# Attention's reciprocal sums: broadcast through memory instead of by matmul with the unit matrix

## The chip, the cores and the metric
The kernel runs on one core of one Trainium2 chip. The metric is the device time of one execution in microseconds, the median of several runs. PE is the matmul engine, DVE the vector engine, ACT the scalar engine, POOL the GpSimd engine, and SP the engine whose queue issues all transfers of this kernel.

## The reference, cut to what matters
One inference step of a hybrid diffusion backbone with two layers: first latent attention beside a convolution branch, then a bidirectional state space mixer. There are 256 context tokens and 1024 latent tokens; everything is fp32. The change concerns the attention of the first layer, 8 heads of width 64. Context queries see the 256 context keys, latent queries see 1536 (512 cached and 1024 own):

```python
s = (einsum('bqhd,bkhd->bhqk', qn, k_nope) + einsum('bqhr,bkr->bhqk', qr, k_rope)) * ATTN_SCALE
p = softmax(s, axis=-1)
attn = einsum('bhqk,bkhd->bqhd', p, v)
mix = concatenate([attn, cv], axis=-1) * silu(gate)
```

The softmax is computed as exp(s - max); the product with v is taken of the exponentials, and the result is multiplied by the reciprocal of each query's sum and by the gate.

## The kernel before
Attention works on head pairs p (4 of them) and query blocks b of 256 tokens (5; b = 0 is the context). A pair and a block make a group, 20 in all; a group has four units (j, qi): head j of the pair, 128 queries qi. All matmuls of scores are three fp32r products (lines 119 to 121, called from a helper), which stand for one product of full precision.

For each unit, u_scores makes the scores with the queries on partitions (one to three tiles of up to 512 keys), takes row maxima on DVE (line 617), the exponentials on ACT with their row sums (line 626), and the reciprocal of the sum, ri, one number for each partition (lines 630, 631, 633). One unit later, u_trans transposes the exponentials on PE (line 646), 128 keys at a time, and copies them out of PSUM (lines 650 and 652). u_values runs for a group after the first unit of the next group has been transposed: it multiplies with v (line 666), with the values' features on partitions and the queries along the row. There the reciprocals are needed along the row, the same on 64 partitions. Before the change PE makes this turn: for each of the four units the column ri, repeated 64 times, is the stationary operand, and the unit matrix is the moving one (line 661). The result goes to the second half of the PSUM tile of the group, po. Then DVE makes t2 = gate x reciprocals (line 671) and om = values x t2 (line 672), and om is stored (line 673). There is one po tile at a time.

Other work runs in this stretch. When the last unit of a pair is through its scores, prep_pair makes the next pair's keys and queries: it loads kh and kl (lines 570, 571) and query weights, and POOL makes the low part ql of the queries (line 588). A convolution branch, conv_norm, is fed in step by step and uses POOL for products and sums of up to 128x1024. The gate tile sg of a group is loaded ahead (line 705; two buffers, freed by t2). After attention the output projection follows on PE, in PSUM tiles that attention frees.

The order of the instructions on each engine isn't that of the text: the compiler's planner lays it out with a simulated timeline (schedule_with_timeline_sim=True in kernel()), and each engine, and SP's queue, then runs its list in order. An instruction that waits holds up those behind it on the same engine.

Of the kernel before, what the change touches and what calls it, by code (L numbers as in the profile page):

```python
# [10 lines left out]
F32 = mybir.dt.float32  # L11
# [39 lines left out]
def body(nc, tc, d, dbg=None, stop=None):  # L51
    es = ExitStack()
    with es:
        _body(nc, tc, d, es, dbg or {}, stop)


def _body(nc, tc, d, es, dbg, stop):
    V, S, G, PE = nc.vector, nc.scalar, nc.gpsimd, nc.tensor
    dma = nc.sync.dma_start

    def pool(name, bufs=1, space=None, side=None, stack=es):
        kw = {}
        if space is not None:
            kw["space"] = space
        if side is not None:
            kw["side"] = side
        if space is None:
            kw["reuse_waits"] = "tile"
        return stack.enter_context(tc.tile_pool(name=name, bufs=bufs, **kw))
# [5 lines left out]
    sm = pool("sm", bufs=3, side="left")  # L75
# [9 lines left out]
    dp = pool("dp", space=DRAM)  # L85

    def psum(tag="x"):
        tag = tag if tag in ptags else "sd"
        p, n = ptags[tag]
        return p.tile([128, 512], F32, name="ps" + tag, tag=tag, bufs=n)  # L90
# [5 lines left out]
    ident = cp.tile([128, 128], F32, name="ident")  # L96
# [21 lines left out]
    def mm3(ps, lh, ll, rh, rl, start, stop_):  # L118
        PE.matmul(ps, lh, rh, start=start, stop=False)  # L119
        PE.matmul(ps, lh, rl, start=False, stop=False)  # L120
        PE.matmul(ps, ll, rh, start=False, stop=stop_)  # L121
# [378 lines left out]
    ap_ = pool("attn", bufs=2, side="right", stack=esB)  # L500
# [92 lines left out]
    for p in range(4):  # L593
        for b in range(5):
            for j in range(2):
                for qi in range(2):
                    units.append((p, b, j, qi))

    def u_scores(u, kq):
        p, b, j, qi = u  # L600
        ks, qs = kq
        tok = (0 if b == 0 else 256 + 256 * (b - 1)) + 128 * qi
        ci = 0 if tok < 256 else (1 if tok < 768 else 2)
        o = tok - CHUNKS[ci][0]
        segs = [0] if b == 0 else [1, 2, 3]
        qh, ql = qs[(j, ci)]
        mx = sm.tile([128, 4], F32, name="mx", tag="mx", bufs=6)
        sums = sm.tile([128, 4], F32, name="sums", tag="sums", bufs=6)
        nk = sum(KSEG[si][1] for si in segs)
        prob = ap_.tile([128, 1536], F32, name="prob", tag="prob")  # L610
        pss = []
        for x, si in enumerate(segs):
            n = KSEG[si][1]
            kh, kl = ks[(j, si)]
            ps = psum("s")
            mm3(ps[:, :n], qh[:, o:o + 128], ql[:, o:o + 128], kh[:, :n], kl[:, :n], True, True)
            V.tensor_reduce(mx[:, x:x + 1], ps[:, :n], axis=AX.X, op=ALU.max, negate=len(segs) == 1)  # L617
            pss.append((ps, n))
        if len(segs) > 1:
            nm = sm.tile([128, 1], F32, name="nm", tag="nm", bufs=6)  # L620
            V.tensor_reduce(nm, mx[:, :len(segs)], axis=AX.X, op=ALU.max, negate=True)  # L621
        else:
            nm = mx[:, 0:1]
        c = 0
        for x, (ps, n) in enumerate(pss):
            S.activation(prob[:, c:c + n], ps[:, :n], AF.Exp, bias=nm, accum_out=sums[:, x:x + 1])  # L626
            c += n
        ri = sm.tile([128, 1], F32, name="ri", tag="ri", bufs=8)
        if len(segs) > 1:
            V.tensor_reduce(ri, sums[:, :len(segs)], axis=AX.X, op=ALU.add)  # L630
            V.reciprocal(ri, ri)
        else:
            V.reciprocal(ri, sums[:, 0:1])
        return prob, ri, nk

    def u_trans(u, st, pts):
        p, b, j, qi = u
        prob, ri, nk = st
        for g in range(0, nk // 128, 4):
            n4 = min(4, nk // 128 - g)  # L640
            if qi == 0:
                pts[(j, g)] = ap_.tile([128, 4, 256], F32, name="ptile", tag="pt", bufs=7)
            dst = pts[(j, g)]
            ps = psum("pt")
            for x in range(n4):
                PE.transpose(ps[:, x * 128:(x + 1) * 128], prob[:, (g + x) * 128:(g + x + 1) * 128], ident)  # L646
            o = dst[:, :n4, qi * 128:qi * 128 + 128]
            p3 = ps[:, :n4 * 128].rearrange("p (k q) -> p k q", q=128)
            if g == 4:
                V.tensor_copy(o, p3)  # L650
            else:
                S.copy(o, p3)  # L652
        pts[("r", j, qi)] = ri

    def u_values(p, b, pts):
        q0 = 0 if b == 0 else 256 + 256 * (b - 1)
        kts = list(range(2)) if b == 0 else list(range(2, 14))
        po = psum("po")
        for qi in range(2):
            for j in range(2):  # L660
                PE.matmul(po[64 * j:64 * j + 64, 256 + 128 * qi:384 + 128 * qi],
                          pts[("r", j, qi)].to_broadcast([128, 64]), ident, start=True, stop=True)
        for x, kt in enumerate(kts):
            for j in range(2):
                h = 2 * p + j
                PE.matmul(po[64 * j:64 * j + 64, 0:256], vt[:, kt, 64 * h:64 * h + 64],  # L666
                          pts[(j, 4 * (x // 4))][:, x % 4, :], start=x == 0, stop=x == len(kts) - 1)
        t2 = ap_.tile([128, 256], F32, name="t2", tag="t2")
        sg = sgs.pop((p, b))
        om = ap_.tile([128, 256], F32, name="om", tag="om")  # L670
        V.tensor_mul(t2, sg, po[:, 256:512])
        V.tensor_mul(om, po[:, 0:256], t2)
        dma(mixd[p, :, q0:q0 + 256], om)

# [25 lines left out]
    for i in range(len(units) + 2):  # L700
        if i < len(units):
            u = units[i]
            if i % 4 == 0:
                sgs[u[:2]] = ap_.tile([128, 256], F32, name="sg", tag="sg")
                dma(sgs[u[:2]], sgd[u[0], :, 256 * u[1]:256 * u[1] + 256])
            state[u] = u_scores(u, kqs[u[0]])
            if i % 20 == 19 and u[0] < 3:
                kqs[u[0] + 1] = prep_pair(u[0] + 1)
        if 0 < i <= len(units):
            v = units[i - 1]  # L710
            pts = done.setdefault((v[0], v[1]), {})
            u_trans(v, state.pop(v), pts)
            if v[2] == 1 and v[3] == 1:
                late_v.append(v)
        if i % 4 == 1 and late_v:
            v = late_v.pop(0)
            u_values(v[0], v[1], done.pop((v[0], v[1])))
        if ci < len(cn) and i % 20 in (1, 3, 5, 7, 9, 11, 13):
            next(cn[ci])
            ci += 1  # L720
        if i == 68:
            esE.close()
            esA.close()
            wps[0] = pool("wpB", bufs=2, side="left")
            hls.append(pool("hlB0", bufs=16, side="left", stack=esH))
            load_mix(0, KORD[:4])
            wao.extend(split_w(d["wao"][m], 8, 128) for m in range(2))
# [161 lines left out]
    def dtile(name, dt=F32, tag=None):  # L889
        return dq.tile([128, HT], dt, name=name, tag=tag or name)  # L890
# [40 lines left out]
    p = dtile("p")  # L931
# [43 lines left out]
    for half in range(2):  # L975
        hs = slice(half * 64, half * 64 + 64)
        for c0 in range(0, 5):
            c = half * 5 + c0
# [561 lines left out]
```

## Time and profile before

| | |
|---|---|
| median of 3 runs | 2057.92 us (2056.36 to 2061.26) |
| the profiled execution | 2060.95 us |
| its span, first to last instruction | 2059.1 us |
| PE busy, share of the span | 1993.4 us, 97% |
| DVE, ACT, POOL busy | 69%, 43%, 28% |
| mean granted clock of PE | 0.988 |
| attention, from the first scores to the last om | 381 to 797 us |

The profiled execution is one run; its time is the span and a little around it. Busy time of PE is the union of matmuls that overlap each other in the pipeline, so the times of single matmuls add up to more than the stretch that they take. The chain of waits goes back from the last instruction and puts each moment down to the one piece of work that everything then hung on.

### The profile page before, as it was taken

The numbers are of one execution on the slowest core, as the hardware profiler recorded it, in microseconds if no ns is written. First come the engines' busy times: TensorE is split into PE (matmuls) and PEld (weight loads), VectorE is DVE, ScalarE is ACT, GpSimd is POOL, SyncE is SP. The second block draws the span as 40 slices with busy tenths as digits, with TensorE's granted clock in tenths as the row PEclk, the third lists the DMA queues.
The fourth block names the chain that finished last, engine by engine and source line by source line (L and its number), as shares of the span: only waits on it lengthen the run. The fifth ranks groups of instructions, "written<-read, shape, count | busy, mean of one in ns | idle before, by whom it ended". The sixth has DMA issues, their size and how long they took to land.

```text
span 2059.1 us, 32474 instructions
## 1 busy us (share of the span) xinstructions
PE 1993.4 (97%) x11830; PEld 1626.0 (79%) x11830; DVE 1415.9 (69%) x2257; ACT 882.3 (43%) x1683; POOL 578.7 (28%) x487
## 2 busy tenths in 40 slices
PE   6999999999999999989999999999999999799997
PEld 3787888777777777868888888888888888589997
DVE  5798798556666673275757876876778587784744
ACT  5411321666566673244544343443334244333531
POOL 1211122212222311563123333333433243342001
PEclk8999999999999999999999999999999999999998
DMA  8434213311122224331566768765866678755442
GB/s 315 181 118 150 54 70 108 115 57 42 57 60 60 77 82 164 140 114 52 142 217 205 229 203 237 208 191 173 244 204 194 179 235 252 220 182 185 145 157 72
DMA packets 273341, 313.57 MB, mean 152 GB/s; under 512 B 21184, under 2 KB 221920, under 8 KB 273184
## 3 DMA queue, kind: packets, MB, share of 16 engines
q1 hardware_dynamic: 273184, 311.51, 48.0%
q8 instruction: 94, 1.54, 0.3%
q14 instruction: 63, 0.52, 0.1%
HBM read 223.38 MB, written 88.05 MB: 151 GB/s over the span
## 4 chain that ended last, share of the span: by engine, by line
PE 90%; DVE 3%; DMA 2%; ACT 1%; issue 1%; SPq 1%; POOL 0%; DVEq 0%; ACTq 0%; POOLq 0%
PE psmm L119 18%; PE psmm L120 18%; PE psmm L121 18%; PE pspo L666 5%; PE pspt L646 4%; PE pssd L1078 3%; PE pss L119 3%; PE pssd L1159 3%; PE pss L121 3%; PE pss L120 3%; PE pssd L1164 2%; PE pssd L1136 2%; PE pssd L1139 2%; PE psx L229 1%; PE pstm L1036 1%
## 5 line engine op out<-in xcount | busy, mean ns | idle before, releaser
L119 PE MATMUL psmm<-hl,wh 128*128 128x512 f32 (+1 forms) x1152 | 428.1, 372 | 4.7 <-ACT wh L114 3.5
L121 PE MATMUL psmm<-hl,wl 128*128 128x512 f32 (+1 forms) x1152 | 423.5, 368 | 4.3 <-POOL wl L115 4.3
L120 PE MATMUL psmm<-hl,wh 128*128 128x512 f32 (+1 forms) x1152 | 423.3, 367 | 0.0
L115 POOL TENSOR_TENSOR wl<-ws,wh 128x1024 fp32r<-128x1024 f32 x89 | 223.6, 2514 | 516.7 <-ACT wh L114 424.5
L119 PEld LDWEIGHTS psmm<-hl,wh 128*128 128x128 f32 x1152 | 219.1, 190 | 37.6 <-ACT wh L114 4.5
L121 PEld LDWEIGHTS psmm<-hl,wl 128*128 128x128 f32 x1152 | 218.8, 190 | 36.9 <-POOL wl L115 6.2
L120 PEld LDWEIGHTS psmm<-hl,wh 128*128 128x128 f32 x1152 | 218.8, 190 | 29.6 <-issue 0.7
L383 DVE SCALAR_TENSOR_TENSOR cacc<-cvin,acw,cacc 128x1295 f32<-128x1295 f32 x120 | 206.9, 1740 | 4.6 <-ACT cacc L378 3.1
L114 ACT CAST wh<-ws 128x1024 fp32r<-128x1024 f32 x109 | 113.6, 1043 | 199.6 <-PE psmm L120 140.3
L848 DVE SCALAR_TENSOR_TENSOR cy<-raw,prm,cy 128x1282 f32<-128x1282 f32 x96 | 157.2, 1637 | 24.6 <-ACT cy L845 17.0
L120 PE MATMUL psmm<-hlo,wh 128*128 128x512 f32 (+3 forms) x480 | 172.1, 359 | 0.0
L119 PE MATMUL psmm<-hh,wh 128*128 128x512 f32 (+3 forms) x480 | 167.8, 360 | 2.5 <-ACT hh L259 2.0
L121 PE MATMUL psmm<-hh,wl 128*128 128x512 f32 (+3 forms) x480 | 170.1, 357 | 0.0
L617 DVE TENSOR_REDUCE mx<-pss 128x1 f32<-128x512 f32 (+1 forms) x208 | 137.3, 668 | 35.2 <-PE pss L121 34.2
L1083 POOL TENSOR_TENSOR st<-st,dec_bc 128x256 f32<-128x256 f32 x104 | 84.3, 815 | 245.2 <-DVE st L1085 165.9
L119 PE MATMUL psmm<-yh,wh 128*128 128x256 f32 (+1 forms) x476 | 147.8, 314 | 5.2 <-ACT yh L1203 3.1
L120 PE MATMUL psmm<-yl,wh 128*128 128x256 f32 (+1 forms) x476 | 148.0, 312 | 0.4 <-DVE yl L1204 0.4
L121 PE MATMUL psmm<-yh,wl 128*128 128x256 f32 (+1 forms) x476 | 147.1, 313 | 0.0
L626 ACT ACTIVATE prob<-pss,nm 128x512 f32<-128x512 f32 x192 | 130.3, 693 | 16.1 <-DVE nm L621 14.2
L646 PE MATMUL pspt<-ident,prob 128*128 128x128 f32 x800 | 121.7, 278 | 4.9 <-ACT prob L626 3.9
L652 ACT COPY ptile<-pspt 128x512 f32<-128x512 f32 (+1 forms) x144 | 81.2, 569 | 104.8 <-PE pspt L646 104.0
L646 PEld LDWEIGHTS pspt<-ident,prob 128*128 128x128 f32 x800 | 92.1, 141 | 40.4 <-ACT prob L626 10.2
(337 smaller groups left out, 4084.5 us busy)
## 6 DMA issues: line engine op xcount, KB each, us to landing
xa<-cmb SPq DMA_DIRECT2D x80, 384.0 KB
wm<-in_wmod_dram SPq DMA_DIRECT2D x48, 512.0 KB
ws<-in_wc_dram SPq DMA_DIRECT2D x40, 512.0 KB
eb<-eyd SPq DMA_DIRECT2D x160, 128.0 KB
ws<-in_wco_dram SPq DMA_DIRECT2D x32, 512.0 KB
cmb<-xt SPq DMA_DIRECT2D x24, 640.0 KB
bx<-cmb SPq DMA_DIRECT2D x72, 192.0 KB
eb<-cmb SPq DMA_DIRECT2D x80, 128.0 KB
```

Of the source, the lines that this page charges most:

```text
L114: S.copy(wh, ws)
L115: (eng or G).tensor_sub(wl, ws, f32(wh))
L119: PE.matmul(ps, lh, rh, start=start, stop=False)
L120: PE.matmul(ps, lh, rl, start=False, stop=False)
L121: PE.matmul(ps, ll, rh, start=False, stop=stop_)
L383: V.scalar_tensor_tensor(cacc[i], cv[:, k:k + CO], acw[:, 31 * i + k:31 * i + k + 1], cacc[i], ALU.mult, ALU.add)
L617: V.tensor_reduce(mx[:, x:x + 1], ps[:, :n], axis=AX.X, op=ALU.max, negate=len(segs) == 1)
L626: S.activation(prob[:, c:c + n], ps[:, :n], AF.Exp, bias=nm, accum_out=sums[:, x:x + 1])
L646: PE.transpose(ps[:, x * 128:(x + 1) * 128], prob[:, (g + x) * 128:(g + x + 1) * 128], ident)
L666: PE.matmul(po[64 * j:64 * j + 64, 0:256], vt[:, kt, 64 * h:64 * h + 64], pts[(j, 4 * (x // 4))][:, x % 4, :], start=x == 0, stop=x == len ...
L848: V.scalar_tensor_tensor(y, raw[:, k:k + RO], ccw[:, 5 * blk + k:5 * blk + k + 1], y, ALU.mult, ALU.add)
L1083: G.tensor_mul(n.rearrange("p (h e) -> p h e", e=64), s.rearrange("p (h e) -> p h e", e=64), dec_ap(u, dr, c))
```

## The change
The reciprocals of a group's four units are now columns of one tile of 128x4. When the last of them is there, SP stores the tile to memory transposed (each column becomes a row of 128 numbers), and two loads bring it back, each repeating one head's 256 numbers on 64 partitions, into a tile rb of 128x256. The four matmuls of line 661 are gone, and t2 is made on POOL from two SBUF tiles instead of on DVE from SBUF and PSUM.

```diff
+    rgs = {}
+    rid = dp.tile([20, 4, 128], F32, name="rid")
...
-        ri = sm.tile([128, 1], F32, name="ri", tag="ri", bufs=8)
+        if (j, qi) == (0, 0):
+            rgs[p, b] = sm.tile([128, 4], F32, name="ri", tag="ri", bufs=3)
+        ri = rgs[p, b][:, 2 * j + qi:2 * j + qi + 1]
         if len(segs) > 1:
             V.tensor_reduce(ri, sums[:, :len(segs)], axis=AX.X, op=ALU.add)
             V.reciprocal(ri, ri)
         else:
             V.reciprocal(ri, sums[:, 0:1])
-        return prob, ri, nk
+        if (j, qi) == (1, 1):
+            g = 5 * p + b
+            dma(rid[g].rearrange("c q -> q c"), rgs[p, b])
+            rb = rgs[p, b] = ap_.tile([128, 256], F32, name="rb", tag="rb")
+            for x in range(2):
+                dma(rb[64 * x:64 * x + 64], rid[g, 2 * x:2 * x + 2].rearrange("c q -> (c q)").unsqueeze(0)
+                    .to_broadcast([64, 256]))
+        return prob, nk
...
-        for qi in range(2):
-            for j in range(2):
-                PE.matmul(po[64 * j:64 * j + 64, 256 + 128 * qi:384 + 128 * qi],
-                          pts[("r", j, qi)].to_broadcast([128, 64]), ident, start=True, stop=True)
...
-        V.tensor_mul(t2, sg, po[:, 256:512])
+        G.tensor_mul(t2, sg, rgs.pop((p, b)))
         V.tensor_mul(om, po[:, 0:256], t2)
```

The tile rb has two buffers.

## Rows read from the trace of the kernel before

**Rows 1.** Page, part 1: busy us (share of the span) xinstructions.
```profile
PE 1993.4 (97%) x11830; PEld 1626.0 (79%) x11830; DVE 1415.9 (69%) x2257; ACT 882.3 (43%) x1683; POOL 578.7 (28%) x487
```

**Rows 2.** Windows: us, then PE, PEld, DVE, ACT, POOL busy (instructions), PEclk, DMA, GB/s.
```profile
530.00:550.00 20.00, 20.00 (x133) 13.86 (x131) 11.47 (x28) 12.24 (x32) 5.93 (x5) 1.00 0.02 7
...
381.00:797.00 416.00, 406.50 (x2583) 291.94 (x2581) 263.92 (x648) 260.08 (x646) 96.02 (x68) 1.00 0.19 57
```

**Rows 3.** Chain of waits, 381 to 797 us: shares by line.
```profile
by line: PE pspo L666 23.5%; PE pspt L646 21.9%; PE pss L119 14.7%; PE pss L121 12.7%; PE pss L120 12.6%; PE pspo L661 4.0%; ACT prob L626 2.4%; DMA wsq<-in_wuq_dram 1.2%; issue 1.0%; ACT ct L550 0.9%; PE pspt L539 0.6%; DVE mx L617 0.6%; D
```

**Rows 4.** Groups by line, 381 to 797 us: busy us, mean ns, idle before.
```profile
L661 PE MATMUL pspo<-ident,ri 128*64 128x128 f32 x160 | 25.4, 297 | 0.7 <-DVE ri L631 0.7
...
L671 DVE TENSOR_TENSOR t<-sg,pspo 128x256 f32<-128x256 f32 x20 | 8.4, 421 | 34.7 <-PE pspo L666 34.7
...
L543 POOL TENSOR_TENSOR la<-la 128x256 f32<-128x256 f32 x5 | 3.7, 731 | 0.4
```

**Rows 5.** Chain of waits, one group: start us, us, what.
```profile
529.69 0.44 PE pspt L646 x4
...
531.03 0.36 PE pspo L661 x2
531.39 0.59 PE pspt L646 x4
...
534.96 0.37 PE pspo L661 x4
...
538.88 0.25 PE pspo L661
```

**Rows 6.** Chain of waits, the end of attention.
```profile
790.61 5.34 PE pspo L666 x46
...
795.97 0.43 DVE t L671
...
796.99 0.36 PE psmm L119
```

**Rows 7.** Timeline of DVE: last reciprocal of a group, and its t2.
```profile
391.98 0.21 DVE L633 RECIPROCAL ri<-sums 128x1 f32<-128x1 f32 x2
...
394.66 0.42 DVE L671 TENSOR_TENSOR t<-sg,pspo 128x256 f32<-128x256 f32 x1 [0.62 <-PE pspo L666]
...
454.47 0.15 DVE L631 RECIPROCAL ri<-ri 128x1 f32<-128x1 f32 x1
...
465.51 0.42 DVE L671 TENSOR_TENSOR t<-sg,pspo 128x256 f32<-128x256 f32 x1 [2.08 <-PE pspo L666]
...
475.51 0.16 DVE L631 RECIPROCAL ri<-ri 128x1 f32<-128x1 f32 x1
...
492.49 0.42 DVE L671 TENSOR_TENSOR t<-sg,pspo 128x256 f32<-128x256 f32 x1 [0.80 <-PE pspo L666]
...
788.71 0.16 DVE L631 RECIPROCAL ri<-ri 128x1 f32<-128x1 f32 x1
```

**Rows 8.** Transfers: decd by tile (ns, start), a load in the chain, the page's packets.
```profile
L972 SPq DMA_DIRECT2D decd<-dece x1: 332/332/332, 1000.7 to 1000.7; - x1
L973 SPq DMA_DIRECT2D dec_bc<-decd x1: 319/319/319, 1002.1 to 1002.1; - x1
...
595.80 2.14 DMA kl<-krd
...
q1 hardware_dynamic: 273184, 311.51, 48.0%
```

**Rows 9.** Timelines of SP, DVE and POOL at the seam before pair 2.
```profile
577.50 0.97 SPq L571 DMA_DIRECT2D kl<-krd  x1
...
580.72 0.16 DVE L631 RECIPROCAL ri<-ri 128x1 f32<-128x1 f32 x1
...
584.52 0.73 POOL L588 TENSOR_TENSOR ql<-qq,qh 128x256 fp32r<-128x256 f32 x1 [41.13 <-ACT qh L587]
...
595.22 0.44 SPq L570 DMA_DIRECT2D kh<-krd  x1
```

More of the change, by code (lines that the diff above doesn't have):

```diff
@@ L633, in u_scores @@
             V.reciprocal(ri, sums[:, 0:1])
-        return prob, ri, nk
+        if (j, qi) == (1, 1):
[6 more added lines that the diff above has]
+        return prob, nk
     def u_trans(u, st, pts):
         p, b, j, qi = u
-        prob, ri, nk = st
+        prob, nk = st
         for g in range(0, nk // 128, 4):
@@ L652, in u_trans @@
                 S.copy(o, p3)
-        pts[("r", j, qi)] = ri
     def u_values(p, b, pts):
```

## The prediction, made before the change was run
> **What bounds the kernel now.** I read the page's busy shares first: PE is busy for 97% of the span, and no other engine is above 69%, PE's weight load apart [rows 1]. So time is lost or won on PE unless something makes PE wait. The change touches only attention, which runs from 381 to 797 us. There PE is busy for 406.5 of 416 us at a granted clock of 1.00, which is the 2.4 GHz level; DVE has 263.9, ACT 260.1, POOL 96.0 [rows 2]. In a stretch of whole units, of 1536 keys (530 to 550 us), PE is busy for all 20 us, DVE for 11.5, ACT for 12.2. Third, the chain of waits of the same stretch: it is almost wholly PE, and the broadcasts of line 661 hold 4.0% of it [rows 3], which is 0.04 x 416 = 16.6 us. The 9.5 us in which PE idles lie mostly where a new head pair is prepared and where the short units (256 keys) run. So I expect PE work that goes to be worth nearly its place in the chain, and the question is what the round trip through memory makes late.
>
> **The work that goes.** Line 661 is 80 matmuls (20 groups, four each); an fp32 matmul of this shape stands as two records, hence x160 [rows 4]. Their 25.4 us of busy time overlap each other and the neighbours, so I don't use them; I use steps of the chain. In the group at 530 to 540 the four broadcasts come in three insertions: 0.36 us, 0.37 us, and one beside the values, 0.25 us [rows 5], together 0.98. Twenty groups at that price would be 19.6 us. The chain has 16.6, so some 17 groups' worth (16.6 / 0.98) is on the path and the rest fills time in which PE waits anyway. Taken: 16.6.
>
> An insertion costs a little more than its own step. Four transposes right behind one take 0.59 us in the chain, four elsewhere 0.44 [rows 5]: 0.15 more, at two of three insertions, in 17 groups: 5.1 us. That is the upper end; the lower is nothing, since those transposes may next stand behind other work and pay the same there. No row says which is nearer, so I take half, 2.5.
>
> DVE loses 20 multiplications of line 671, 8.4 us [rows 4]. They are off the path, with one exception: after the last group PE has nothing left and the chain runs over t2 (0.43 us), om, and then the first matmul of the output projection [rows 6]. There t2 can be ready before the values are. That is 0.4 us gained, once. If t2 came late there, the loss would be as large as its lateness.
>
> **The work that comes.** POOL gets 20 products of 128x256. POOL's 128x256 product takes 0.73 us [rows 4]: 14.6 us on an engine that is busy for 96 of 416. Its cover is that idle time. Where the cover is thin, at the three seams between head pairs, POOL makes the low half of q (line 588) on which DVE and the next scores wait; the first of them at one seam starts at 584.52, and the group's last reciprocal was at 580.72 [rows 9]. If the planner puts t2 ahead of such a step and the broadcast is not there yet, q is late by t2 and by the wait.
>
> The queue of SP gets 60 transfers. The issue of a small store or load holds it for 0.32 to 0.33 us [rows 8], so 20 us in 416, in a queue that stands empty for long: at that seam nothing is issued between 577.50 and 595.22 [rows 9], and the three transfers fall right there. The two loads wait for the store at the head of the queue; behind them stand the next group's gate tile sg, the store of om, and at the seams the key halves kh and kl. By the rows none of these is needed within a few us of that moment, so I cost SP at nothing; gone, the cover would cost a key load's lateness at three seams, some 3 x 2 us.
>
> **How late is the broadcast?** From the last reciprocal of a group: (a) store to load. The nearest row is the one small round trip there is, decd: the store is issued at 1000.7, the load that waits for it at 1002.1, 1.4 us [rows 8]. That store has runs of 20 bytes; the new one writes its four columns transposed, so each run is 4 bytes, 512 of them if each is a packet of its own. The page's packets took 48.0% of 16 engines' span for 273184 [rows 8], 0.480 x 16 x 2059.1 / 273184 = 0.058 us each; 512 of them over 16 engines are 1.9 us more. Bounds: nothing more, and twice that. (b) second issue: 0.45 with its gap. (c) landing: the load of 64 KB in the chain at the seam took 2.14 us [rows 8], and each new load also writes 64 KB. (d) t2 on POOL, 0.73. Sum 1.4 + 1.9 + 0.45 + 2.14 + 0.73 = 6.6 us, between 4.7 and 8.5.
>
> The Trainium skill (DMA: Bandwidth & Descriptors, section "Rules for kernel authors") speaks against this store: a non-contiguous last dimension lowers to one descriptor per element. Whether the 4-byte runs go so, no row shows; by that rule the upper half of my interval is the likelier one, 6.6 to 8.5, and the sum below loses at most its 3 us again.
>
> What time is there? From the last reciprocal to the start of today's t2 it is 11.0 to 17.0 us in 15 groups (smallest and largest in [rows 7]), because the values of a group run after the transposes of the next unit and are spread between them. In five groups it is less: 2.7, 5.5, 6.9, 7.1 and 7.3 us, the first and the last of the 20 groups among them [rows 6, 7]. At 6.6 us two groups are late, by 3.9 and 1.1. Then om waits at the head of DVE, behind it the row maxima of the next scores, and PE runs dry when its score banks are full. The engines' orders are laid out by a planner that knows of the round trip, so om may stand later and the wait cost nothing.
>
> These hazards together lie between nothing and some 12 us (5.0 on DVE for the two groups; 0.73 plus 1.6, which is t2 plus about half of the interval of the round trip, at three seams, 7.0). POOL and SP are idle for most of the time and 18 groups have room, so I take 3.
>
> **Sum.** -16.6 - 2.5 - 0.4 + 3.0 = -16.5 us. The profiled execution has 2060.95 us (span 2059.1 and 1.85 around it), which would become 2044.5; it lies 3.0 above the median of the runs shown, 2057.92, and that becomes 2041.4. With the ends: -16.6 - 5.1 - 0.4 = -22.1 gives 2035.8; -16.6 - 0.4 + 12 = -5.0 gives 2052.9, of which I count what lies above 2050 to the first rival.
>
> **Rivals.**
> *Part of the gain is swallowed.* PE comes sooner to the next unit and waits there for its softmax, or a seam is late. For it: PE's idle time in the stage is made of such waits, and it would only have to double, 9.5 us more. Against it: in whole units ACT and DVE are busy for some 12 of 20 us, so 5% less PE work leaves them room. -19.5 + 9.5 to 14 gives 2048 to 2053; the part above 2050 is this case.
> *No change.* The broadcasts were mostly filler, or the gain is eaten by seams and by a new order of the instructions: all 9.5 us of idle again and a store at the upper bound. 2054 to 2062. Against it: 16.6 us stand in the chain itself.
> *Slower.* One mechanism: the round trip is longer than the room, and om blocks DVE in every group it is late in. With 10 us from reciprocal to t2 the five short groups are late by 7.3, 4.5, 3.1, 2.9 and 2.7, together 20.5, and the gain before hazards (19.5) is gone: that is the point from which it decides. With 12 us they lose 30.5 and the others 3.7: 34.2 - 19.5 = 14.7 slower, 2072.6. For it: nothing in the trace shows a store of 4-byte runs. Against it: even the double price ends at 8.5 us.
> *More than counted.* The planner, freed of the broadcasts, also closes waits at the seams: below 2036.
>
> **How the numbers follow.** Likeliest, 2036 to 2050: 0.60. Swallowed in part, 2050 to 2054: 0.14. No change: 0.11. Slower, up to 2080: 0.10. Below 2036: 0.05. The predicted time is that of the sum, 2041.4. A measurement of this kernel can tell about 0.2% (4.1 us) from no change, so faster means under 2053.8: 0.60 + 0.14 + 0.05 = 0.79; same 0.11; slower 0.10. The range leaves out what lies below 2036 (0.05), the slower case (0.10) and the upper half of no change (0.05): 2036 to 2058.
>
> **What would show it.** Right: no matmul of line 661 is left, PE's busy time in attention is some 20 us less, and the stage is shorter by 15 to 20 us with PE still at 97% or more of it; the broadcast's loads are issued 1.5 to 5 us after their store; t2 on POOL ends before the values in nearly all groups; after attention the stages last as long as before. Wrong: om or DVE's maxima wait for t2 or for the loads for several us in many groups; the first scores of a head pair wait for ql behind a t2 on POOL; PE's idle time in the stage rises from 9.5 to 20 us or more; or a stage after 797 us changes by several us, which would be the planner's order and not the broadcast.

## The result: 4.2% slower, and the profile after

The changed kernel takes 2147.06 us (median of 4 runs, 2142.94 to 2156.57) beside 2059.59 for the kernel before (4 runs): a ratio of 1.0425 [1.0405, 1.0444]. The forecast was 2041.4 with a range of 2036 to 2058. The sign is wrong, and the time lies far above even the rival that ended on the slow side.

Line numbers after the change: the last reciprocal is line 636, the store of ri to rid 641, the loads of rb 644, t2 678 on POOL, om 679 on DVE. First the page's busy shares of the changed kernel:

```profile
PE 2003.4 (94%) x11670; PEld 1631.2 (76%) x11670; DVE 1402.8 (66%) x2237; ACT 883.4 (41%) x1683; POOL 591.3 (28%) x507
```

The 160 records of line 661 are gone (11830 to 11670), yet PE is busy for 10 us more, at a lower mean granted clock (0.976 against 0.988), and for a smaller share of a longer span [rows 1]. The windows (columns as in [rows 2]; the second one holds all of attention) and the group of om by line, whose start times mark where attention ends:

```profile
381.00:797.00 416.00, 353.78 (x2049) 253.73 (x2050) 212.66 (x538) 219.97 (x548) 97.59 (x78) 0.94 0.21 50
376.00:876.00 500.00, 418.40 (x2436) 299.39 (x2435) 252.18 (x628) 261.50 (x647) 110.84 (x88) 0.93 0.22 53
...
L679 DVE TENSOR_TENSOR om<-pspo,t x20: 411/425/426, 399.5 to 873.6; 128x256 f32<-128x256 f32 x20
```

The last om starts at 873.6; before, the last t2 started at 795.97 and om followed it [rows 6]. So attention ends some 77 us later, out of 82.1 us of longer span; the 4.9 left over come behind it (more on them at the end of the account of the prediction). In the same 416 us PE is now busy for 353.8 instead of 406.5. The granted clock is 0.94 there instead of 1.00: PE pauses in every group, and part of the stretch runs below the 2.4 GHz level.

The chain of waits of attention names the cause:

```profile
by line: DMA rid<-ri 29.2%; DMA rb<-rid 13.2%; PE pspo L673 6.7%; PE pspt L658 6.7%; DVE mx L620 5.5%; PE pss L119 5.0%; PE pss L120 3.7%; PE pss L121 3.6%; ACT prob L629 3.4%; issue 3.0%; POOL t L678 2.4%; DMA hl<-mixd 1.6%; POOL ql L588 1
```

It was almost wholly PE [rows 3]. Now 42.4% of it is the round trip's store (rid<-ri) and loads (rb<-rid). One group, from the timelines of SP, POOL, DVE and PE of the changed kernel (start us, us; in brackets the idle time before and what ended it):

```profile
536.79 0.16 DVE L636 RECIPROCAL ri<-ri 128x1 f32<-128x1 f32 x1
536.98 0.37 SPq L641 DMA_DIRECT2D rid<-ri  x1
...
545.11 3.62 SPq L644 DMA_DIRECT2D rb<-rid  x2
...
550.82 0.73 POOL L678 TENSOR_TENSOR t<-sg,rb 128x256 f32<-128x256 f32 x1 [10.08 <-DMA rb<-rid]
...
551.58 0.33 SPq L712 DMA_DIRECT2D sg<-sgd  x1
551.59 0.42 DVE L679 TENSOR_TENSOR om<-pspo,t 128x256 f32<-128x256 f32 x1 [6.09 <-POOL t L678]
```

From the store's issue to the loads' issue it is 8.13 us, from there to t2 5.71, and from the reciprocal to om 14.8, where the forecast had 6.6 to the end of t2. DVE stands 6.09 us at om and POOL 10.08 us at t2. Summed over attention, the waits of POOL, DVE, SP and PE (us in total, times, longest):

```profile
POOL t L678 <- DMA rb<-rid: 268.7, 19, 29.8
...
DVE om L679 <- POOL t L678: 82.0, 14, 11.9
POOL ql L588 <- ACT qh L587: 46.5, 15, 10.9
DVE qq L586 <- POOL ql L588: 42.2, 13, 10.2
...
SPq L644 <- DMA rid<-ri: 159.1, 20, 10.0
...
PE pss L119 <- DVE qq L586: 14.1, 3, 5.3
```

Three in-order queues stand for the round trip: SP at the loads (159.1 us), POOL at t2 (268.7), DVE at om (82.0). That a queue stands doesn't yet say that it costs: a queue can also stand because it has nothing else to do. Through POOL's low part ql, needed by qq on DVE, it also reaches the first scores of a head pair (14.1 us on PE).

### The profile page after: what moved, and what is told of

Its sections match the earlier page's. It is cut to its first block, busy times and chain, and to the rows that moved or that the text cites. A ratio compares the mean times of both kernels' runs of the same rounds, so it can differ in the third digit from the quotient of the medians.

```text
span 2141.2 us, 32259 instructions
## 1 busy us (share of the span) xinstructions
PE 2003.4 (94%) x11670; PEld 1631.2 (76%) x11670; DVE 1402.8 (66%) x2237; ACT 883.4 (41%) x1683; POOL 591.3 (28%) x507
## 2 busy tenths in 40 slices
DMA packets 287102, 316.23 MB, mean 148 GB/s; under 512 B 32384, under 2 KB 235680, under 8 KB 286944
## 3 DMA queue, kind: packets, MB, share of 16 engines
q1 hardware_dynamic: 286944, 314.18, 47.2%
## 4 chain that ended last, share of the span: by engine, by line
PE 76%; DMA 13%; DVE 6%; ACT 2%; POOL 2%; issue 1%; SPq 1%; DVEq 0%; POOLq 0%; ACTq 0%
PE psmm L119 18%; PE psmm L120 17%; PE psmm L121 17%; DMA rid<-ri 7%; DMA rb<-rid 3%; PE pssd L1085 3%; PE pssd L1166 3%; PE pssd L1171 2%; PE pssd L1143 2%; PE pspo L673 2%; PE pspt L658 2%; PE pssd L1146 2%; PE pss L119 1%; DVE mx L620 1%; PE psx L229 1%
## 5 line engine op out<-in xcount | busy, mean ns | idle before, releaser
L119 PE MATMUL psmm<-hl,wh 128*128 128x512 f32 (+1 forms) x1152 | 429.6, 373 | 11.5 <-DVE raw L820 7.3
L658 PE MATMUL pspt<-ident,prob 128*128 128x128 f32 x800 | 121.3, 282 | 14.1 <-ACT ptile L664 8.8
L673 PE MATMUL pspo<-ptile,vt 128*64 128x256 f32 x800 | 118.6, 401 | 6.1 <-DVE om L679 5.7
```

## The experiments

Every ratio is to the kernel before, run beside it on the same chip (its medians there lie between 2060.4 and 2062.7 us). Line numbers differ from run to run. Three questions: what about the round trip costs, who stands for it, and why the matmuls' removal gave nothing back.

### What about the round trip costs?

**Runs of 16 bytes.** Each partition's four numbers go out as one piece, 128 pieces in place of 512. The values come back permuted, so the product differs. The order of instructions on PE, DVE, ACT and POOL is that of the changed kernel.

```diff
-            dma(rid[g].rearrange("c q -> q c"), rgs[p, b])
+            dma(rid[g].rearrange("c q -> (c q)").rearrange("(q c) -> q c", c=4), rgs[p, b])
```

> The changed kernel, but the store of a group's 128x4 reciprocals goes out as it stands, 128 runs of 16 bytes in place of 512 runs of 4 bytes; the loads are the same, so the reciprocals come back in another order (this changes the values, not the amount of work). Theory A (the store's 4-byte runs make the round trip long: 8.1 to 10.5 us from the store's issue to the loads' issue in the trace of the changed kernel): the store takes about a quarter, 2 to 3 us, om waits hardly any more, and the time falls from 2147 to 2040-2065. Theory B (any round trip of two transfers is too long for the place that the planner gives om): the store is shorter, but om still waits; 2090-2140. Theory D (the queue of SP is held up and key loads come late): 2100 or more, with waits for kh and kl.

2058.32 us (10 runs), 0.9985 [0.9975, 0.9996]. The whole loss is gone, by the store's layout alone. SP's timeline for one group, and DVE's wait at om over the stage:

```profile
530.28 0.33 SPq L641 DMA_DIRECT2D rid<-ri  x1
531.70 1.09 SPq L644 DMA_DIRECT2D rb<-rid  x2
...
DVE om L679 <- POOL t L678: 1.7, 2, 1.5
```

The store takes 1.42 us, what decd took [rows 8], and om's wait falls from 82.0 us to 1.7. Theory A, the long store, holds.

**Runs of 16 and of 8 bytes, computed rightly.** The first has one load of all 512 numbers on 128 partitions and t2 in two halves of POOL; the second has two columns in a piece, 256 pieces.

```diff
-    rid = dp.tile([20, 4, 128], F32, name="rid")
+    rid = dp.tile([20, 128, 4], F32, name="rid")        # 16 bytes
+    rid = dp.tile([20, 2, 128, 2], F32, name="rid")     # 8 bytes
...
```

> A version with 16-byte runs that gives the right result: the store goes out as it stands, one load brings a group's 512 numbers (2 KB) to all 128 partitions, and POOL multiplies in two halves, picking every fourth number. Theory A: the store takes 1.4 us as in e1_runs16 and om does not wait, 2052-2064, no better than the kernel before by more than 0.4%. Theory B would have shown in e1_runs16 already. The load is twice as large and POOL has 40 products in place of 20, so if POOL or the load matter: 2065-2080.

> As the changed kernel, but the store writes 256 runs of 8 bytes (a head's two columns side by side), and POOL picks every second number; the result is right. If a run costs the same whatever its size (theory A: 8.1 us for 512, 1.4 us for 128), the store takes about 3.6 us, the reciprocals are back some 8.5 us after the last reciprocal, and only the short groups are late: 2058-2072. If only 4-byte runs are slow, the store takes 1.4 to 2 us and the time is that of e1_runs16, 2052-2062.

2066.54 us (11 runs), 1.0023 [1.0014, 1.0032], and 2068.46 (7 runs), 1.0032 [1.0022, 1.0043]. So also the forms with the right result come to within 0.4% of the kernel before, and neither beats it. The first lies where its expectation had it if POOL or the larger load matter; the second lies where a price by the piece would put it. With 256 pieces the loads follow the store after 3.25 us:

```profile
540.02 0.36 SPq L641 DMA_DIRECT2D rid<-ri  x1
543.27 1.09 SPq L644 DMA_DIRECT2D rb<-rid  x2
```

**Number or order of the pieces?** 512 pieces of four bytes again, but laid partition by partition, eight bytes apart, instead of column by column. The loads fetch other data, ones among them. Apart from one memset, PE, DVE, ACT and POOL keep the changed kernel's order.

```diff
-            dma(rid[g].rearrange("c q -> q c"), rgs[p, b])
+            dma(rid[g].rearrange("q (c s) -> q c s", s=2)[:, :, 0], rgs[p, b])
...
```

> The changed kernel with the 512 four-byte pieces of the store laid partition by partition, eight bytes apart, instead of column by column; a store of ones fills that memory once ahead of attention, and the loads read 1 KB of it each, so what is multiplied is not the broadcast. Theory 1, the number of pieces sets the price: the loads are issued 7 to 9 us after the store as before, and the time is 2135 to 2155 us. Rival, the column order sets it: 3 to 5 us, and 2062 to 2085 us.

2079.70 us, 1.0099 [1.0066, 1.0132]. SP's timeline (one group) and its waits at the loads:

```profile
541.99 0.56 SPq L644 DMA_DIRECT2D rid<-ri  x1
546.97 1.10 SPq L647 DMA_DIRECT2D rb<-rid  x2
...
SPq L647 <- DMA rid<-ri: 72.2, 20, 4.6
```

With as many pieces the store takes 3.4 to 6.0 us in place of 8.1 to 10.5. The rival holds: most of the loss, 2147.06 - 2079.70 = 67 us, comes with the column order, in which one partition after the other fills adjacent four-byte words, and 2079.70 - 2058.32 = 21 us is what 512 pieces cost more than 128 even so. The run changes the order and puts gaps between the words, both at once; which of the two makes the difference isn't shown.

**Loads that don't depend on the store.** The store of 512 pieces stays; the loads read rows of an input, so what is multiplied isn't the broadcast.

```diff
-                dma(rb[64 * x:64 * x + 64], rid[g, 2 * x:2 * x + 2].rearrange("c q -> (c q)").unsqueeze(0)
+                dma(rb[64 * x:64 * x + 64], d["xT"][128 * x + g, 0:256].unsqueeze(0)
```

> The changed kernel, but the two loads read rows of an input instead of the stored reciprocals, so nothing waits for the store; store, loads and POOL's product stay as they are (the values differ). Theory A and B (the wait is what costs): the time falls to 2035-2055, below the kernel before by what the matmuls were worth. Theory E (the stores themselves disturb other transfers, 10240 small packets): it stays above 2070.

2068.57 us, 1.0047 [1.0029, 1.0066]. This lies between the two expectations. The slow stores, when nothing waits for them, cost at most some 8 us of the 86 or so. The waiting is what costs. (The order of the instructions differs in places from the changed kernel's.)

**A store of four long rows.** One PE transpose a group turns ri into 4 x 128, ACT copies it out of PSUM, and the store has four runs of 512 bytes. In a second run the copy is on DVE.

```diff
-            dma(rid[g].rearrange("c q -> q c"), rgs[p, b])
+            pr = psum("pt")
+            PE.transpose(pr[0:4, 0:128], rgs[p, b], ident)
+            rt = ap_.tile([4, 128], F32, name="rt", tag="rt", bufs=1)
+            S.copy(rt, pr[0:4, 0:128])     # second run: V.tensor_copy
+            dma(rid[g], rt)
```

> The changed kernel with one TensorE transpose a group that turns ri (128 x 4) into 4 x 128, a ScalarE copy of it out of PSUM, and a store of four rows of 512 bytes in place of 512 pieces of four bytes; the loads, t2 and om stay. Theory 1, the store is the whole loss: the round trip falls to some 1.5 (store) + 5 us and the time to 2056 to 2066 us, beside 2058 of the run with 16-byte runs. Rival, the extra hop through TensorE and ScalarE costs TensorE's order (20 transposes that wait for ri): 2066 to 2080 us.

> The run with the transposed store, with the copy of 4 x 128 out of PSUM on VectorE in place of ScalarE. Theory 1, ScalarE's 28 us of standing at that copy delayed its exps and so TensorE at the scores' tiles (47 us of waits there): 2058 to 2072 us. Rival, the 20 transposes cost TensorE's order whoever copies: 2078 to 2088 us.

2083.55 us, 1.0103 [1.0087, 1.0119], and 2084.17, 1.012 [1.0095, 1.0145]. The store takes 1.18 us, and still 21 and 24 us are lost, more than either expectation of the first run allowed. Who copies makes no difference, so theory 1 of the second run, ACT's standing, fell; its time lies in the rival's range. PE's own waits of the first of the two:

```profile
PE pss L119 <- ACT prob L629: 15.6, 17, 1.9
PE pspt L642 <- DVE ri L636: 7.0, 13, 3.7
```

PE waits 7.0 us for ri at its own transposes, and 15.6 us for exp at the scores' PSUM tiles, where the run with 16-byte pieces has 5.9. The two together are 16.7 us more than there; what links them was not settled. (The 47 us in the second expectation add the waits of PE's weight load to PE's own; the two stand in part for the same moments.)

### Who stands for it?

**t2 back on DVE.** If POOL at t2 were the trouble, this would help.

```diff
-        G.tensor_mul(t2, sg, rgs.pop((p, b)))
+        V.tensor_mul(t2, sg, rgs.pop((p, b)))
```

> The changed kernel with the product of gate and reciprocals on DVE instead of POOL. If the loss came from POOL standing at t2 (268.7 us of waiting, q's low half behind it): the time falls to 2100-2125. If om's wait on DVE is the loss (theories A and B): the same product now waits on DVE itself, 2135-2160.

2204.35 us, 1.0696 [1.0676, 1.0717], slower than both expectations had it: now DVE itself stands at t2, 172.8 us in 18 groups. Here the wait on DVE costs 57 us more than the one on POOL.

**om later, t2 later, the loads later.** Three runs that each keep the store of 512 pieces. In all of them t2 and om are issued two units later, and one more queue's waiting instruction is tied behind row maxima of the next group (red, the last maximum): om; then t2 too; then the loads too, issued one unit later.

```diff
+        if late_o and (i % 4 == 3 or i > len(units)):
+            u_out(*late_o.pop(0), lastred[0])
...
-        V.tensor_mul(om, po[:, 0:256], t2)
+        after(V.tensor_mul(om, po[:, 0:256], t2), red)      # first run
+        after(G.tensor_mul(t2, sg, rgs.pop((p, b))), red)   # second
...
+                after(ld, lastred[0])                       # third
```

> The changed kernel with its 4-byte store, but t2 and om of a group are issued two units later and om is tied behind the row maxima of the next group's last unit, so DVE comes to om some 16 to 20 us after the last reciprocal instead of about 8. If the loss is DVE standing at om (theory A, second half): the store still takes 8 us and the time falls to 2050-2080. If the long store itself, SP's queue or POOL at t2 are the loss: 2110 or more.

> The changed kernel, its store of 512 four-byte pieces kept, with t2 (GpSimd) and om (VectorE) both issued one unit later and behind the row maxima of that unit, so that neither engine stands for the round trip; SyncE's two loads still stand behind the store. Theory 1, three in-order queues stand for the store and each costs: against 2127 with om alone moved, GpSimd's part comes off and SyncE's stays, 2085 to 2115 us. Rival, GpSimd's standing costs nothing: 2122 to 2132 us.

> As the run before, and the two loads are issued one unit later too, behind row maxima that come after the store has landed, so that SyncE's queue does not stand at the loads for the whole store. Store and loads are those of the changed kernel. Theory 1, the loss is only what the queues' heads stand for: 2058 to 2080 us with the 8 us store still there. Rival, the 512 pieces slow the other transfers or the memory itself: no better than the run before within 8 us, and above 2100.

2127.03 us, 1.031 [1.0296, 1.0324]; 2090.24, 1.0139 [1.0124, 1.0155]; 2087.05, 1.0115 [1.0097, 1.0134]. In the first run DVE's wait at om fell to 19.4 us, but 65 of the some 86 us stayed: DVE's standing at om isn't the main loss, and the time lies where the expectation had it if the store, SP's queue or POOL at t2 are. POOL still stands 236.6 us at t2 there. The timelines of POOL, SP and PE show one way in which that reaches PE:

```profile
631.91 0.72 POOL L682 TENSOR_TENSOR t<-sg,rb 128x256 f32<-128x256 f32 x1 [8.06 <-DMA rb<-rid]
632.60 2.38 POOL L554 TENSOR_TENSOR ct<-ct,lb 128x1024 f32<-128x1024 f32 x1
...
635.00 0.38 SPq L555 DMA_DIRECT2D mixd<-ct  x1
...
638.21 0.36 SPq L532 DMA_DIRECT2D ct<-cvd  x1
...
642.99 1.26 POOL L535 TENSOR_TENSOR la<-ct 128x512 f32<-128x512 f32 x1 [8.02 <-DMA ct<-cvd]
...
645.11 1.22 PE L539 MATMUL pspt<-la,ones 128*128 128x256 f32 x2 [6.35 <-POOL la L536]
```

POOL comes to the convolution's product ct only after 8.06 us at t2; SP stores ct and then loads the next one; POOL waits 8.02 us for that load, and PE 6.35 for POOL. Tying t2 too gave 37 us more, so theory 1 of the second run (POOL's standing costs) holds: POOL's wait for the loads fell from 236.6 to 30.7 us, and it now stands at t2 for the row maxima instead. The third run gave only 3 more and missed its range of 2058 to 2080. But it doesn't test SP's standing, because its edit didn't free SP: a unit is shorter than the store (a group of four takes some 22 us in the kernel before, the store 8 and more), and SP stands at the loads nearly as long as before. SP's waits in the second and the third run, and one of PE's own in the third:

```profile
SPq L645 <- DMA rid<-ri: 170.2, 20, 10.7
...
SPq L649 <- DMA rid<-ri: 145.1, 18, 10.9
...
PE pspo L678 <- DVE om L687: 13.0, 6, 4.9
```

So what SP's standing costs is open. The values have one PSUM tile, and om now leaves it late. (The 30 us in the next expectation added the weight load's waits to the matmul's, which stand for the same moments; PE's own are 13.0.)

**om a unit earlier, and two halves for the values.** The first run keeps the late loads and puts t2 and om at i % 4 == 2, one unit earlier, with t2 untied. The second keeps the late places and gives succeeding groups the two halves of po in turn.

```diff
-        if late_o and (i % 4 == 3 or i > len(units)):
+        if late_o and (i % 4 == 2 or i > len(units)):       # first run
...
+        po = pos[0][:, 256 * (nv[0] % 2):256 * (nv[0] % 2) + 256]   # second
```

> The changed kernel with its store of 512 pieces, the loads issued one unit later behind row maxima as in the run before, and t2 and om two units after the group's last score, om tied behind that unit's maxima and t2 not tied at all. Theory 1, the 25 us left over in the run before were TensorE's 30 us of waits at om, made by the edit itself, and the store costs nothing once no queue stands for it: 2056 to 2070 us. Rival, the 512 pieces cost in themselves: 2080 to 2092 us.

> The run with loads, t2 and om all one unit later (2087 us), with the values of succeeding groups written in turn into the two halves of one 128 x 512 PSUM tile (in the kernel before the second half held the broadcast reciprocals), so that TensorE may start the next group's values while om has not read the last ones. The store of 512 pieces stays. Theory 1, the store costs nothing when neither SyncE, GpSimd, VectorE nor TensorE stands for it: 2056 to 2070 us, and TensorE's 30 us of waits at om are gone. Rival, the pieces cost in themselves: 2080 to 2090 us.

2125.4 us, 1.0318 [1.0291, 1.0345]: DVE stands again at om for t2, 51.4 us, and POOL at t2; both expectations were missed. 2079.91, 1.0093 [1.0076, 1.011], with 9.4 us on PE at om instead of 13.0: theory 1 missed, the rival at its lower edge. Neither run tests what theory 1 says, since SP stands for the store in the second as well:

```profile
SPq L650 <- DMA rid<-ri: 132.4, 18, 10.1
```

No place was found for om that is free while the store takes 8 us. Of the some 86 us, 67 came back by moving om and t2 and by the two halves; 18 stay, with 9.4 us of PE's waits at om and SP's standing among them. The run whose loads don't wait for the store bounds what the pieces cost in themselves: at most 8 us.

### Why did the matmuls' removal give nothing?

**No broadcast at all.** No matmuls, no trip; t2 on POOL takes a tile that is there anyway (vt), so what is multiplied isn't the reciprocals.

```diff
-            dma(rid[g].rearrange("c q -> q c"), rgs[p, b])
...
-        G.tensor_mul(t2, sg, rgs.pop((p, b)))
+        G.tensor_mul(t2, sg, vt[:, 0, 0:256])
```

> No broadcast at all: no matmuls with the unit matrix, no store, no loads; POOL multiplies the gate with a tile that lies in SBUF anyway (the reciprocals are left out of the result). This is what the removed matmuls are worth. By the prediction's sum without its hazards 2040 (16.6 to 22.1 us less than before). If the matmuls were only filler in PE's idle time: 2055-2060.

2063.12 us (10 runs), 1.0004 [0.9993, 1.0015]. With nothing in its place, the removal is worth nothing. The time fits the second expectation, the filler, better than the first (it is 3 us above its range). Against the kernel before, t2 has moved to POOL here too, and the planner laid the other engines' instructions in a new order; this run can't separate that from the matmuls.

**The matmuls twice and four times**, in the kernel before.

```diff
-        for qi in range(2):
+        for _ in range(2):        # and range(4)
+          for qi in range(2):
```

> The kernel before with each of the 80 broadcast matmuls issued twice. If PE's work sets the pace (the prediction's first term): 16 to 20 us more, 2075-2082. If PE has room for them, as e3_no_broadcast suggests (without them 2063, the same as before): 2056-2066.

> The kernel before with its four broadcast matmuls a group issued four times over into the same place (320 instead of 80). Theory 1, each set of 80 costs its own busy time on TensorE: three more sets are three times the 11 us that one more set cost, 2092 to 2098 us. Theory 2, the first sets fall into waits that TensorE has anyway and only what does not fit there costs: the third and fourth set cost their full share of the chain, 16.6 us each, so 2073 + 33 = 2106 us, within 5. Below 2085 would say that even four sets are partly hidden.

2073.04 us, 1.0052 [1.004, 1.0065], between its two expectations, and 2101.52, 1.0189 [1.017, 1.0208], in the range of theory 2. Against the kernel before, run beside each: 0 to 1 set, nothing (the run above); 1 to 2, 2073.04 - 2061.95 = 11 us; 2 to 4, (2101.52 - 2062.50) - 11 = 28, or 14 each. So the first set falls into waits that PE has without it, the second in part.

**exp that doesn't wait for the row maxima**, with the matmuls and without broadcast. The bias is a constant and the scale 0.001, so this is no softmax of the scores; the maxima are still made.

```diff
-            S.activation(prob[:, c:c + n], ps[:, :n], AF.Exp, bias=nm, accum_out=sums[:, x:x + 1])
+            S.activation(prob[:, c:c + n], ps[:, :n], AF.Exp, bias=zb, scale=0.001, accum_out=sums[:, x:x + 1])
```

> The kernel before, its 80 matmuls kept, with exp's bias a constant in place of the negated row maximum and its scale 0.001 (the maxima are still computed and read by nothing): so ScalarE can start on a score tile as soon as it is written. Both theories: faster than before or equal, 2040 to 2062 us. It is the base for the run after it.

> The same constant bias and scale in the kernel without broadcast matmuls and without the trip through memory (t2 takes an input tile). Theory 1, the loop from scores over maxima and exp back to the scores' PSUM tiles eats the gain: with the loop shortened the removal of 80 matmuls shows, 10 to 20 us below the run with constant bias and matmuls. Rival, the matmuls cost nothing in themselves: within 4 us of it.

2062.87 us, 1.0017 [1.0003, 1.003], with the matmuls; 2051.37, 0.9956 [0.9942, 0.997], without: now the removal is worth 11.5 us, as theory 1 had it. Windows of 381 to 797 us, first of the kernel without broadcast and real maxima, then of the two with free exp (with matmuls, without), each with PE's own waits at the scores' PSUM tiles for exp. In the first fence that wait in the kernel before stands ahead, and two more waits of PE follow:

```profile
PE pss L119 <- ACT prob L626: 1.3, 4, 0.6
...
381.00:797.00 416.00, 397.40 (x2426) 286.85 (x2425) 255.63 (x628) 259.70 (x646) 111.58 (x88) 0.99 0.19 57
...
PE pss L119 <- ACT prob L629: 5.0, 9, 1.0
PE pss L119 <- DVE qq L586: 3.9, 1, 3.9
PE pspt L651 <- ACT ptile L657: 3.8, 11, 1.2
```

```profile
381.00:797.00 416.00, 406.33 (x2572) 289.95 (x2572) 259.90 (x642) 259.50 (x646) 95.75 (x67) 0.99 0.19 56
...
PE pss L119 <- ACT prob L629: 0.3, 1, 0.3
```

```profile
381.00:797.00 416.00, 403.23 (x2488) 293.35 (x2487) 254.87 (x631) 261.45 (x649) 112.50 (x88) 0.99 0.21 65
...
PE pss L119 <- ACT prob L632: 2.0, 2, 1.4
```

Without broadcast PE is idle for 416 - 397.40 = 18.6 us where it was 9.5 before [rows 2]: 9.1 more. Of these, 3.7 are waits at the scores' PSUM tiles, which exp must have read before new scores go in; the others stand mostly at the transposes' PSUM tiles (3.8 where it was 0.2) and at one head pair's queries (3.9 where there was none), while the transposes' wait for exp got shorter. When exp needn't wait for the maxima, PE's idle time without broadcast falls to 416 - 403.23 = 12.8 us, and attention ends sooner: the last om starts at 785.60 instead of 796.00 us. Where attention starts, PE idles and its granted clock falls from the 2.4 GHz level, by an amount that differs from run to run: from 380 to 400 us PE is busy for 15.2 us at a mean of 0.74 without broadcast, for 16.5 at 0.91 before, and for 17.7 at 1.00 with 16-byte pieces. So the stretch from the second om to the last compares better. The second om, before, without broadcast, and with free exp with matmuls and without:

```profile
422.51 0.42 DVE L672 TENSOR_TENSOR om<-pspo,t 128x256 f32<-128x256 f32 x1
...
424.14 0.42 DVE L673 TENSOR_TENSOR om<-pspo,t 128x256 f32<-128x256 f32 x1 [3.21 <-PE pspo L666]
...
421.42 0.42 DVE L675 TENSOR_TENSOR om<-pspo,t 128x256 f32<-128x256 f32 x1
...
422.32 0.42 DVE L676 TENSOR_TENSOR om<-pspo,t 128x256 f32<-128x256 f32 x1 [2.35 <-PE pspo L669]
```

The last one starts at 796.42, 796.00, 796.66 and 785.60. So the stretch is 373.9 us before and 371.9 without broadcast, 2.0 less (it is 370.9 in the run with 16-byte pieces); with free exp it is 375.2 and 363.3, 12.0 less. The wait of exp for the maxima is therefore what kept most of the gain from showing: it lengthens the loop from scores over maxima and exp back to the PSUM tiles, and the broadcasts stood in PE's gaps. That the new order of the instructions has no part in it isn't shown.

## Why the prediction was wrong, point by point

**Store to load, term (a): mis-sized, and this made the sign.** The sum had 1.4 + 1.9 = 3.3 us, 5.2 at most. It measured 8.1 to 10.5, and with a store of 1.4 us the whole loss is gone. That there is one packet for each piece was right. The page's queue lines, of the changed kernel and of the runs with 16 and 8 bytes:

```profile
q1 hardware_dynamic: 286944, 314.18, 47.2%
```

```profile
q1 hardware_dynamic: 279264, 314.18, 49.3%
```

```profile
q1 hardware_dynamic: 281824, 314.18, 49.4%
```

From 16-byte runs to four-byte runs there are (286944 - 279264) / 20 = 384 packets more a group, which is 512 - 128; to eight-byte runs 128 more, 256 - 128. This agrees with the rule of the Trainium skill (DMA: Bandwidth & Descriptors, "Rules for kernel authors") that a non-contiguous last dimension gives one descriptor per element. But the time that I made of it, 6.6 to 8.5 us for the whole trip, was half of what came, because the price of a packet was an average over packets of mostly 512 bytes and more (21184 of 273341 are smaller). 128, 256 and 512 pieces took 1.4, 2.9 and 8.1 us (the shortest of 20 groups each), and the last figure fell to 3.4 with another order: neither number nor bytes alone gives the price.

**Landing, term (c): too small.** 2.14 us from one undisturbed load, with the second issue, term (b), 2.59; from the loads' issue to t2 it was 3.2 to 5.7 us. Term (d), 0.73, was exact.

**POOL and SP as idle engines that cost nothing: wrong for POOL, open for SP.** "POOL and SP are idle for most of the time and 18 groups have room, so I take 3" was the price of all hazards. Both are in-order queues, and both stood: moving om gave 20 us, and taking POOL's wait for the loads away 37 more. "So I cost SP at nothing" isn't tested: SP stood 159.1 us, and no run with the slow store freed it alone. The mechanism at the seams that I named (ql late behind t2) is there, 42.2 us on DVE at qq and 14.1 on PE; I had priced it at 7.0 at most, with 1.6 for half of an interval that is 3.8 wide.

**The slow rival: its mechanism was right in part, its chance and size were not.** Its deciding point was a trip of 10 us; the trip from the reciprocal to the end of t2 was 13 to 15 (once 16.6). By its own sum, over the 20 distances in the trace before, a trip of 14 us makes 66 us of lateness, 47 us slower after the gain: about half of the loss. It counted om on DVE alone, and more of the loss came back with POOL than with om. It counted the lateness of om against today's t2, but the new order puts om elsewhere: with the same order and a fast store, reciprocal to om is 6.3 to 16.6 us, and with the slow one DVE stands at om in 14 of 20 groups. What I held against it, "even the double price ends at 8.5 us", was an end of the range made from a mean, not from a row of such a store.

**The work that goes: -16.6 and -2.5 measured about 0** (2063.12 against 2060.96 with everything removed). The step that failed is that PE work which goes would be "worth nearly its place in the chain". A chain counts PE as the path wherever it is busy; it doesn't show how soon behind it the next wait would end. Here 9.1 us became new idle time. Another part is at the start of attention, where the run without broadcast makes its first om 2.6 us later, at a granted clock of 0.74 against 0.91 (380 to 400 us); the rest I can't place. The rival "No change" said it: "The broadcasts were mostly filler", at a chance of 0.11. The rival that the gain is swallowed named one of the places, PE waiting for a unit's softmax. What it was refused with, "in whole units ACT and DVE are busy for some 12 of 20 us, so 5% less PE work leaves them room", was the wrong argument: freeing exp of the maxima brought 12 us with ACT and DVE as busy as with them (261.5 and 254.9 us against 259.7 and 255.6), so what held was the length of the loop, not their load.

**Stages behind attention: a sign of being wrong that came.** From the last om to the end of the span it takes 2059.1 - 796.4 = 1262.7 us before and 1267.6 after. It is 1267.6 also without broadcast and with the matmuls issued twice, and 1263 to 1269 in the other runs. So these 5 us don't belong to the round trip. The prediction put such a change down to the planner's order; no run here shows its cause.

**The end, -0.4:** not seen; the last group's t2 came late as all others.

## What to carry to other kernels

Price a store by its pieces in the order in which they lie in memory, and when no row has that shape, leave the upper end open: ask at which length the trip decides, and how sure it is that it is shorter. A round trip through memory costs at the heads of in-order queues, so look at the instruction that waits for it on each of them. When an edit is meant to free a queue, read that queue's waits after it: the run is only a test if they are gone. Before you book removed work of a busy engine as gain, ask which loop it waits in next; doubling the work tells its price in one direction only.

## What the runs showed of the hardware that was not expected

512 four-byte pieces took from 8.1 us column by column and from 3.4 us partition by partition with gaps; 128 pieces of 16 bytes took from 1.4 us and four of 512 bytes 1.2. The Trainium skill (DMA: Bandwidth & Descriptors, "Specifications") says that a transfer under 512 bytes makes the engine read, modify and write. That would fit a price that hangs on which words lie beside each other, but the pieces of 16 bytes are under 512 bytes too and were fast, and no run here shows the mechanism.
